# One PSUM bank moved from the input projections to the transposes of the band attention's first two blocks

## The chip, the cores and the metric

The kernel runs on one core of one Trainium2 chip. The metric is device microseconds (us) of one execution; of several executions the median is taken. The kernel before takes 3063.79 us (median of 3 executions, 3062.14 to 3065.21).

## The reference

One inference step of a one-layer streaming encoder, over 2048 prompt tokens and 32 sample tokens (model width 1024). Attention has two groups: group A is differential attention over all earlier keys, group B is band attention in chunks of 64 frames, each of which sees itself and the eight chunks before it. The band attention of the prompt:

```python
qa, ka, va, qb, kb, vb = split_proj(rmsnorm(hp, g_attn[i]), w_in[i])
oa = diff_attn_prompt(qa, ka, va, t5_table, lam)
ob = band_attn_prompt(qb, kb, vb, band_table[i])
hp = hp + merge(oa, ob, subln_g[i], out_norm_b[i], w_out[i], lam_init)
hp = ffn_ple(hp, p_prompt[i], g_mlp[i], w_up[i], w_down[i], w_ple_gate[i], w_ple_proj[i])
...
def band_core(q, k, v, bias, mask):
    s = jnp.einsum('bqhd,bkhd->bhqk', q, k).astype(jnp.float32) * (HEAD_DIM ** -0.5) + bias[None]
    s = jnp.where(mask, s, NEG)
    p = jax.nn.softmax(s, axis=-1)
    return jnp.einsum('bhqk,bkhd->bqhd', p.astype(v.dtype), v)
```

Everything is fp32. The kernel splits each operand into a high and a low part and adds three products (high by high, high by low, low by high), so a product of depth 1024 is 24 matmuls.

## The kernel before, in words

**Blocks and stages.** Tokens are handled in four blocks b = 0 to 3 of 512 (the last has 544: 512 prompt tokens and the 32 sample tokens). `proj` (L443) makes the q, k and v of a group: `vtile` (L411) makes a 128x256 piece of v (tile `vps`, 24 matmuls of 256 columns, read out by ScalarE at L427), the loop at L451 to L502 makes a piece of q or k (tile `qps`, 24 matmuls of 512 columns, for b = 3 two tiles of 272 columns each; read out by VectorE at L475 or L480). q, k and v are written to DRAM and read back by the attention. `run` writes the stages down in this order: projections of blocks 0 and 1, attention A of the first 1024 queries (`attn_a`), group B's projections of blocks 0 and 1, band attention of its first two blocks, group B's projections of block 2 and of block 3, band attention of its last two blocks, group A's projections of blocks 2 and 3 (`proj_a`), then the norm of the band attention's outputs (`onorm`, two of them woven into the end of `proj_a`), the load of the normed attention outputs of block 0 (`oload`), attention A of the last queries, the output projections (`outproj`, tile `ops`) and the MLP (tiles `ups` and `dps`).

**What sets the order.** The kernel is built with a scheduler (`schedule_with_timeline_sim=True`). The order in which the program is written is only a priority: on each engine the scheduler places what its own estimate of time says is ready, the earlier-written first. Once placed, each engine's instructions run in that order, and so do the DMA issues, which all stand on SyncE's queue (SP). So projections written later stand between the attention's instructions on TensorE (PE) as filler.

**Band attention.** `attn_b` (L715) is called for four blocks `JB` of the queries: (0, 1), (2, 3), (4, 5) and (6, 7, 8). It runs over 8 heads; a head has four tiles of 128 queries (the last block also the 32 sample queries). For each query tile `first` (L796) does the scores (tile `sb`, L804; two banks of 320 keys where there are 640, two matmuls each), bias and maximum on VectorE (L807), the exponential and the scaling on ScalarE (L812, L814). `second` (L817) transposes the 128x640 weights on PE (tile `tpb`, L826: five transposes in two banks, four and one), copies each bank out as a high part on ScalarE (L834) and a low part on VectorE (L835), and after two query tiles `attn_b_out` (L842) multiplies by the values (tile `ob`, L856) and adds up into `t` (L859 to L861), which is written to the DRAM tensor `oT` once per head. From the second block on, a head has 16 matmuls into `sb`, 20 into `tpb` and 12 into `ob`, so counts of `sb` matmuls are used below to say how far the band attention is: the first block ends at 64, the second at 192, all four at 464.

**What follows the projections.** `onorm` (L868) reads the four `oraw` tiles of a block back from `oT`, squares them on ScalarE (L875, L877) and adds; `colnorm2` sums over partitions with two matmuls (tile `css`, L1046 and L1047), makes the factor `r` (L1050 to L1056) and writes it to DRAM (`rB`). `oload` (L881) reads eight `oraw` tiles of block 0, multiplies the last four by `rb` (read from `rB`; L902) and splits each into the operands `oact` and `ou` of the output projection (ScalarE L181, VectorE L187). The buffers of `oact` lie where the projections' activations lay, so they come free when the projections that read these are done; the `oraw` buffers are a ring of three.

**PSUM.** There are 8 banks: two in the pool `mm` (`mz`), one in the pool `mmx`, two for scores (`ps_s`), two for transposes (`ps_t`), one for outputs (`ps_o`), all eight in use. `Rings` (L109) is an object with a `tile` method that takes the next pool of its list at each call. `mm` is such a ring over `mz`, `mz` and `mmx`: everything that is given `mm` goes through three banks.

## Time and profile before

| what | value |
|---|---|
| median of 3 executions | 3063.79 us |
| the profiled execution's own time | 3069.65 us |
| its span, first to last instruction | 3067.9 us |
| PE busy in the span | 2947.2 us |
| VectorE, ScalarE, GpSimd busy | 1830.6, 1746.5, 1887.9 us |
| mean granted TensorE clock | 0.985 |

In the views shown below, a row of the table by stretches gives the stretch in us from the span's start and its length, then for each engine its busy time and its number of instructions in brackets (PE matmuls, PEld weight loads, DVE VectorE, ACT ScalarE, POOL GpSimd), the granted clock of TensorE as a share of full speed, the busy share of the DMA engines and GB/s. With a tile's name only that tile's PE instructions are counted. A row of the order of time has the start, the duration, the engine, the line, the operation, what is written and read, the form, how many rows were merged, and in brackets the idle time before it with what ended that. A matmul's busy time overlaps the next one's, so sums of matmul durations are more than the time they take.

### The profile page before, as it was taken

The page shows a single profiled execution, that of the slowest core. Times are in us where ns is not written, and L with a number is a line of the kernel's source. Part 1 is how long each engine was busy: PE and PEld are TensorE (multiplying, and loading weights), DVE is VectorE, ACT ScalarE, POOL GpSimd, SP SyncE. Part 2 cuts the span into 40 slices and gives each one's busy share as a digit, 9 for nine tenths or more (in the row PEclk, how much of TensorE's full clock was granted, in tenths as well). Part 3 has the DMA queues.
Part 4 walks back from the last instruction along what each step waited for, and adds up shares of the span by engine and source line. Part 5 has one row for each costly group of instructions (what it writes and reads, how often), then busy time and mean ns, then how long its engine had stood idle before and what let it go on. Part 6 is the DMA issues. An engine that isn't in the chain of part 4 may idle for free. (4 is left out here: it accounts for less than half of the span.)

```text
span 3067.9 us, 50404 instructions
## 1 busy us (share of the span) xinstructions
PE 2947.2 (96%) x17409; PEld 2599.0 (85%) x17409; DVE 1830.6 (60%) x4233; ACT 1746.5 (57%) x3234; POOL 1887.9 (62%) x2509
## 2 busy tenths in 40 slices
PE   7999999899789999999999999999899999999997
PEld 6788889899677888888888888879798888999997
DVE  5156554654655555566666565545677885577664
ACT  5256554765666666566666565554555545555455
POOL 3467775324146544656655565777688888787774
PEclk9999999999899999999999999999999999999999
DMA  9878866976687554455655543347433446333331
GB/s 310 250 222 245 241 221 211 262 228 211 190 248 241 147 148 131 145 155 172 198 149 155 150 128 125 118 148 249 136 131 117 148 151 231 122 101 112 102 99 57
DMA packets 298119, 529.54 MB, mean 173 GB/s; under 512 B 36668, under 2 KB 161632, under 8 KB 297864
## 3 DMA queue, kind: packets, MB, share of 16 engines
q1 hardware_dynamic: 297864, 526.32, 55.6%
q8 instruction: 138, 2.26, 0.3%
q14 instruction: 117, 0.96, 0.1%
HBM read 425.19 MB, written 104.97 MB: 173 GB/s over the span
## 5 line engine op out<-in xcount | busy, mean ns | idle before, releaser
L176 POOL TENSOR_TENSOR wl<-wr,wh 128x256 fp32r<-128x256 f32 x648 | 492.8, 792 | 270.2 <-ACT wh L181 230.7
L181 ACT ACTIVATE piece<-wr 128x512 fp32r<-128x512 f32 x406 | 245.8, 625 | 290.4 <-PE ups L220 133.3
L176 POOL TENSOR_TENSOR piece<-wr,piece 128x256 fp32r<-128x256 f32 x404 | 338.0, 863 | 92.3 <-ACT piece L181 85.2
L181 ACT ACTIVATE wh<-wr 128x1024 fp32r<-128x1024 f32 x228 | 240.5, 1055 | 190.8 <-PE ups L220 45.9
L166 POOL TENSOR_TENSOR wl<-wr,wh 128x256 fp32r<-128x256 f32 x264 | 202.9, 799 | 208.4 <-ACT wh L181 202.6
L219 PE MATMUL dps<-uh,piece 128*128 128x272 f32 (+1 forms) x768 | 247.0, 325 | 8.3 <-ACT piece L181 5.0
L221 PE MATMUL dps<-uh,piece 128*128 128x272 f32 (+1 forms) x768 | 247.3, 325 | 1.1 <-POOL piece L166 0.9
L220 PE MATMUL dps<-ul,piece 128*128 128x272 f32 (+1 forms) x768 | 248.1, 324 | 0.1
L166 POOL TENSOR_TENSOR piece<-wr,piece 128x256 fp32r<-128x256 f32 x280 | 235.1, 872 | 18.9 <-ACT piece L181 15.4
L219 PE MATMUL ups<-cs,piece 128*128 128x256 f32 (+1 forms) x864 | 246.2, 285 | 0.0
L221 PE MATMUL ups<-cs,piece 128*128 128x256 f32 (+1 forms) x864 | 246.1, 285 | 0.0
L220 PE MATMUL ups<-cs,piece 128*128 128x256 f32 (+1 forms) x864 | 245.9, 285 | 0.0
L219 PE MATMUL qps<-aH,wh 128*128 128x512 f32 (+1 forms) x640 | 226.9, 355 | 2.0 <-DVE ql L475 2.0
L220 PE MATMUL qps<-aL,wh 128*128 128x512 f32 (+1 forms) x640 | 227.9, 356 | 0.0
L221 PE MATMUL qps<-aH,wl 128*128 128x512 f32 (+1 forms) x640 | 226.5, 354 | 0.0
L1112 DVE TENSOR_TENSOR h<-h,dps 128x512 f32<-128x512 f32 x256 | 173.5, 682 | 80.2 <-PE dps L221 77.0
L638 ACT ACTIVATE e<-e,nm 128x128 f32<-128x128 f32 (+16 forms) x136 | 157.2, 1156 | 108.5 <-DVE nm L636 108.0
L1155 DVE TENSOR_TENSOR h<-h,dps 128x272 f32<-128x272 f32 (+1 forms) x384 | 189.0, 514 | 42.9 <-PE dps L221 42.3
L219 PE MATMUL dps<-uh,wh 128*128 128x512 f32 x512 | 205.7, 402 | 0.6 <-DVE h L1112 0.6
L219 PE MATMUL ups<-cH,wh 128*128 128x512 f32 x512 | 202.5, 396 | 0.0
L221 PE MATMUL ups<-cH,wl 128*128 128x512 f32 x512 | 202.2, 395 | 0.1
L220 PE MATMUL ups<-cL,wh 128*128 128x512 f32 x512 | 202.0, 394 | 0.0
(307 smaller groups left out, 9234.0 us busy)
## 6 DMA issues: line engine op xcount, KB each, us to landing
wr<-w_up SPq DMA_DIRECT2D x128, 512.0 KB, 3.5
wr<-w_down SPq DMA_DIRECT2D x128, 512.0 KB, 3.6
v<-vSa SPq DMA_DIRECT2D x64, 512.0 KB, 4.6
q<-qS SPq DMA_DIRECT2D x128, 256.0 KB, 5.2
wr<-w_qk SPq DMA_DIRECT2D x50, 512.0 KB, 5.2
ka<-kS SPq DMA_DIRECT2D x32, 512.0 KB, 7.1
wr<-w_out SPq DMA_DIRECT2D x32, 512.0 KB, 4.8
wr<-w_ple_gate SPq DMA_DIRECT2D x32, 512.0 KB, 3.5
```

Of the source, the lines that this page charges most:

```text
L166: nc.gpsimd.tensor_tensor(out[:, sl], a[:, sl], b[:, sl], op=op)
L176: nc.gpsimd.tensor_tensor(out[:, sl], a[:, sl], b[:, sl], op=op)
L181: nc.scalar.activation(hi, raw, AF.Copy)
L219: nc.tensor.matmul(ps, lh, rh, start=start and i == 0, stop=False)
L220: nc.tensor.matmul(ps, lh, rl, start=False, stop=False)
L221: nc.tensor.matmul(ps, ll, rh, start=False, stop=stop and i == n - 1)
L638: nc.scalar.activation(row, row, AF.Exp, bias=nmx, accum_out=z[:nr, m : m + 1])
L1112: nc.vector.tensor_tensor(hv, hv, ps, op=ALU.add)
L1155: nc.vector.tensor_tensor(hv, hv, ps, op=ALU.add)
```

## The change

```diff
-            mm = Rings((mz, "mm"), (mz, "mm"), (opened(mmx, "mmx", 1, PSUM), "mm"))
+            third = opened(mmx, "mmx", 1, PSUM)
+            mm = Rings((mz, "mm"), (mz, "mm"), (third, "mm"))
...
+            tb = Rings((ps_t, "tp"), (ps_t, "tp"), (third, "mm"))
             for js in JB[: len(JB) // 2]:
-                self.attn_b(js, bp, ps_s, ps_t, ps_o)
-            weave(self.proj((2,), 1, acts, sg, mm), lifted(self.prep(3, acts, pp, mm, "mm")), 3)
+                self.attn_b(js, bp, ps_s, tb, ps_o)
+            weave(self.proj((2,), 1, acts, sg, mz), lifted(self.prep(3, acts, pp, mz, "mm")), 3)
             ppx.close()
             self.rawp = Rings((self.wp, "wr"))
             self.caches(sg, tp)
-            drain(self.proj((3,), 1, acts, sg, mm))
+            drain(self.proj((3,), 1, acts, sg, mz))
...
             def proj_a():
-                yield from self.proj(HALVES[1], 0, acts, sg, mm, gs=range(GS))
+                yield from self.proj(HALVES[1], 0, acts, sg, mz, gs=range(GS))
                 for b in HALVES[1]:
-                    yield from self.proj((b,), 0, acts, sg, mm, vs=(), gs=range(GS, 4))
+                    yield from self.proj((b,), 0, acts, sg, mz, vs=(), gs=range(GS, 4))
```

In the first two blocks of the band attention (64 query tiles, 96 tiles `tpb`) every third `tpb` goes to the third bank. The projections of blocks 2 and 3, group B's and group A's, and the `rp` tiles of block 3 use the two banks of `mz` alone. The last two blocks of the band attention keep two banks for transposes, and `onorm`, `outproj` and all later stages keep `mm` with three. No instruction is added or removed: both programs have 17404 matmuls on PE, 576 of them into `tpb`, 1920 into `qps`, 1632 into `vps`.

The scheduler places the instructions anew from the stage of attention A's first queries on. Until the band attention begins, the counts are nearly the same (at 16 `sb` matmuls, 1248 `qps` matmuls stand ahead before and 1243 now). Then they part. How many matmuls of each kind stand ahead of a given `sb` matmul on PE:

| `sb` matmuls | `vps` before, now | `qps` before, now | `ops` before, now |
|---|---|---|---|
| 48 | 1309, 1302 | 1344, 1344 | 0, 0 |
| 96 | 1616, 1585 | 1344, 1344 | 0, 0 |
| 112 | 1632, 1632 | 1438, 1364 | 0, 0 |
| 144 | 1632, 1632 | 1668, 1485 | 0, 0 |
| 176 | 1632, 1632 | 1897, 1606 | 0, 0 |
| 192 | 1632, 1632 | 1920, 1671 | 0, 0 |
| 224 | 1632, 1632 | 1920, 1809 | 0, 0 |
| 240 | 1632, 1632 | 1920, 1920 | 72, 0 |
| 320 | 1632, 1632 | 1920, 1920 | 384, 384 |

At the end of the band attention 432 `ups` and 378 `dps` matmuls stood ahead before, 394 and 336 now; at the last matmul of attention A it was 1536 and 1445, now 1488 and 1397. The rows near the end of the program are the same again.

**The end of the projections on PE.** Before, from the last `qps` matmuls on:

```order
L221 MATMUL qps<-aH,wl 128x272
L1046 MATMUL css<-sh,ones_r 128x512
L1047 MATMUL css<-sl,ones_r 128x512
L804 MATMUL sb<-kbt,q 128x320 x4
L856 MATMUL ob<-pb,vbt 128x512 x4
L856 MATMUL ob<-pb,vbt 128x2x128
L826 MATMUL tpb<-ident,eb 128x128 x4
L856 MATMUL ob<-pb,vbt 128x2x128
L826 MATMUL tpb<-ident,eb 128x128
L804 MATMUL sb<-kbt,q 128x320 x4
L826 MATMUL tpb<-ident,eb 128x128 x5
```

Band attention alone goes on like this until 48 `sb`, 59 `tpb` and 36 `ob` matmuls have passed; only then comes the first `ops`. The same place now:

```order
L221 MATMUL qps<-aH,wl 128x272
L804 MATMUL sb<-kbt,q 128x320 x2
L1047 MATMUL css<-sl,ones_r 128x512
L804 MATMUL sb<-kbt,q 128x320 x2
L1046 MATMUL css<-sh,ones_r 128x512
L826 MATMUL tpb<-ident,eb 128x128 x5
L1047 MATMUL css<-sl,ones_r 128x512
L219 MATMUL ops<-oact,wh 128x512
L804 MATMUL sb<-kbt,q 128x320 x4
L220 MATMUL ops<-oact,wh 128x512
```

The first `ops` stands 12 matmuls behind the last `qps`, and both blocks' `css` stand between them (block 0's first one is the exception: it stands some 240 matmuls earlier, its partner L1047 here). After the first `ops` come in turn 4 `sb`, 26 `ops`, a query tile's `ob` and `tpb`, 9 `ops`, two query tiles of the band attention with 3 `ops` between, and then 24 `ops` in a row.

**The end of the second block on SP's queue** (`t_6463` is the output of its last head). Before:

```order
L157 DMA oT<-t_6327 64x512
L157 DMA kbt<-kS 64x1024 x2
L157 DMA q<-qS 64x1024
L157 DMA bb<-dbb 128x640
L157 DMA q<-qS 64x1024
L157 DMA vbt<-vSb 128x8x128
L157 DMA oT<-t_6463 64x512
L157 DMA oraw<-oT 128x512 x3
L157 DMA kbt<-kS 64x1024 x2
```

Now:

```order
L157 DMA oT<-t_6463 64x512
L157 DMA ka_pt<-kr 128x512
L157 DMA kbt<-kS 64x1024 x2
L157 DMA bb<-dbb 128x640
L157 DMA q<-qS 64x1024 x2
L157 DMA kS<-qh 128x512
L157 DMA kS<-ql 128x512
L157 DMA oraw<-oT 128x512 x3
```

Now results of the projections (`ka_pt`, `kS`) are still being written when the second block's last output goes out, and the three `oraw` loads that open the way to the output projection stand behind them.

## The prediction

> **What bounds the kernel now.** I read the page first, then the stretches of the band attention, then who waited there. The page's first lines and its rows of PE and of the clock in 40 slices:

> ```profile
> span 3067.9 us, 50404 instructions
> PE 2947.2 (96%) x17409; PEld 2599.0 (85%) x17409; DVE 1830.6 (60%) x4233; ACT 1746.5 (57%) x3234; POOL 1887.9 (62%) x2509
> PE   7999999899789999999999999999899999999997
> PEclk9999999999899999999999999999999999999999
> ```

> PE is the bound almost everywhere. The change removes no work, so it can only win or lose where PE stands idle or runs at a lowered clock. The eleventh slice (767 to 844 us) is the weak one in the part that the change touches: least busy, and the only digit of the clock under 9. The stretches around it:

> ```profile
> 608.20:644.50 36.30, 35.07 (x267) 33.68 (x267) 22.59 (x87) 23.48 (x51) 4.51 (x10) 0.98 0.85 244
> 669.30:770.00 100.70, 100.70 (x654) 92.73 (x653) 45.84 (x164) 57.92 (x117) 43.00 (x67) 1.00 0.70 210
> 776.00:826.00 50.00, 32.89 (x131) 24.32 (x130) 28.71 (x105) 31.82 (x67) 5.70 (x13) 0.75 0.65 192
> 860.00:890.00 30.00, 23.67 (x114) 19.98 (x113) 14.91 (x44) 16.28 (x30) 16.62 (x25) 0.89 0.91 281
> 890.00:1010.00 120.00, 110.81 (x534) 90.28 (x533) 68.10 (x188) 79.47 (x147) 72.31 (x101) 0.99 0.78 232
> ```

> From 669 to 770 us PE is never idle. From 776 to 826, between the last projection and the first output projection, it is idle for 50.00 - 32.89 = 17.1 us of 50 and has a clock of 0.75: band attention stands there without filler. Call this the hole. PE's waits before it (515 to 776 us, two rows) and in it (776 to 826, three rows):

> ```profile
> PE sb L804 <- DVE stb L807: 5.8, 4, 2.2
> PE tpb L826 <- DVE pb L835: 1.0, 1, 1.0
> ```

> ```profile
> PE ob L856 <- DVE pb L835: 7.3, 3, 6.6
> PE sb L804 <- DVE stb L807: 7.0, 11, 0.9
> PE tpb L826 <- DVE pb L835: 2.4, 2, 1.6
> ```

> Waiting for a bank of the transposes cost PE 1.0 us in 261 us beside the projections. The third bank's direct worth is therefore about nothing. What counts is the order that comes with it.

> **Term 1: the old hole, +30 us.** How long PE needs for the hole's work, if fed, comes from the stretches of `qps` alone (two pure ones, wide and narrow, then the mixed one) and the count of `sb` in two stretches:

> ```profile
> 100.00:120.00 20.00, 20.00 (x88) 1.00 1.05 353
> 515.80:522.80 7.00, 7.00 (x58) 1.00 0.89 239
> 669.30:770.00 100.70, 81.03 (x461) 1.00 0.70 210
> ```

> ```profile
> 669.30:770.00 100.70, 13.47 (x65) 1.00 0.70 210
> 776.00:826.00 50.00, 12.21 (x44) 0.75 0.65 192
> ```

> A 512-column matmul takes 20/88 = 0.227 us, a 272-column one 7/58 = 0.121. `proj_a` has 24 wide for 48 narrow ones, 0.156 on average. So the 461 `qps` took 71.9 us of the 100.7, and the 65/16 = 4.06 heads of band attention beside them 28.8: 7.1 us a head. The hole's 44/16 = 2.75 heads are 19.5 us of work in 50: 30 us are lost, 17.1 idle and the rest as slower matmuls. Now 556 `qps` stand between the 112th and the 240th `sb`, where before 482 ended at the 177th. That fills these heads, so I take all 30 off; at least the 17.1 of idle goes.

> How the clock follows the idle time shows around an earlier, smaller gap:

> ```profile
> 603.00:606.40 3.40, 1.40 (x12) 1.19 (x11) 1.90 (x9) 2.85 (x9) 1.80 (x5) 1.00 0.83 274
> 606.40:609.80 3.40, 3.40 (x14) 2.83 (x13) 1.68 (x6) 1.30 (x4) 3.40 (x5) 0.51 0.11 30
> ```

> After 3.4 us with PE 1.40 busy, the next 3.4 us run at 0.51, although the longest single wait between 515 and 776 us was 2.2: here it is the idle share that lowers the clock, not one long gap. [...]

> **Term 2: the new hole, -13 us.** Now both `css` come at the very end of the projections, and block 0's output projection needs `r` from them for the last four of its eight operands. The chain, from the trace of before (block 0's `css` and its `r`, then block 1's; the two transfers; the first use of `rb` and the first `ops` behind it):

> ```profile
> 773.47 0.39 PE L1047 MATMUL css<-sl,ones_r 128*128 128x512 f32 x1
> 782.89 0.69 DVE L1056 TENSOR_TENSOR r<-r,sqacc 128x512 f32<-128x512 f32 x1
> 831.06 0.60 ACT L1050 ACTIVATE sqacc<-css 128x512 f32<-128x512 f32 x1 [0.75 <-PE css L1047]
> 843.89 0.67 DVE L1056 TENSOR_TENSOR r<-r,sqacc 128x512 f32<-128x512 f32 x1
> 835.09 0.75 DVE L902 SCALAR_TENSOR_TENSOR oraw<-oraw,g_b_s,rb 128x512 f32<-128x512 f32 x1 [0.19 <-DMA rb<-rB]
> 840.79 0.50 PE L220 MATMUL ops<-oact,wh 128*128 128x512 f32 x1 [0.79 <-DVE oact L187]
> ```

> ```profile
> rB<-r SPq DMA_DIRECT2D x3, 256.0 KB, 2.0
> rb<-rB SPq DMA_DIRECT2D x3, 256.0 KB, 3.5
> rB<-r SPq DMA_DIRECT2D x1, 272.0 KB, 5.8
> rb<-rB SPq DMA_DIRECT2D x1, 272.0 KB, 5.4
> ```

> From `css` to `r` it took 9.7 and 13.5 us, writing and reading 2.0 + 3.5 (5.8 + 5.4 the slow ones), from L902 to `ops` 5.7: 20.9 to 24.7 us. Meanwhile PE's order has, before the run of 24 `ops` that needs `rb`, 39 `ops` at 0.227 = 8.9 us and some 3.25 query tiles at 7.1/4 = 5.8, with `css` 15.2. That leaves 5.7 to 9.5 us idle. VectorE stands at L902 too, so the band attention cannot fill it. The old hole lost 30 us for 17.1 idle, 1.75 times; so 10.0 to 16.6, and I take 13. Bounds: 5.7 if the clock stays up, and with the slow transfers (15.2 idle) 26.6.

> **Term 3: thinner filler, -5 us.** Between the 112th and 240th `sb` a head now has 69.5 `qps`, 10.8 us, and takes 10.8 + 7.1 = 17.9 us instead of about 25. The nearest row is 608.20:644.50: 32 `sb`, two heads, 18.15 us each with `vps` as filler, 36.30 - 35.07 = 1.23 us idle. So 0.6 us a head, 8 heads: 4.9 us, where the full heads of 669 to 770 lost nothing. Bounds 0 and twice that. ScalarE and VectorE were 23.48 and 22.59 busy of 36.30 there, so neither is the bound at this pace.

> **Term 4: two banks for the projections, -2 us.** With two, PE fills one while the other is read out. A read-out on VectorE or ScalarE takes:

> ```profile
> L475 DVE SCALAR_TENSOR_TENSOR ql<-qps,rbt x14: 422/434/692, 541.9 to 766.9; 128x272 f32<-128x272 f32 x10, 128x512 f32<-128x512 f32 x4
> L427 ACT ACTIVATE vraw<-vps,rcol x18: 448/472/478, 567.8 to 649.3; 128x256 f32<-128x256 f32 x16, 32x256 f32<-32x256 f32 x2
> ```

> ```profile
> L219 PE MATMUL qps<-aH,wh 128*128 128x512 f32 (+1 forms) x640 | 226.9, 355 | 2.0 <-DVE ql L475 2.0
> ```

> The shortest tile keeps PE busy for 24 x 0.121 = 2.9 us, six times a read-out, so only a queue on the reading engine can hold PE up. With three banks the 640/8 = 80 `qps` tiles lost 2.0 us. 84 tiles now have two: 2.1 us at the same rate. Bounds: 0, and a whole read-out each, 84 x 0.45 = 38 us. I stay at the row, since VectorE was 45.84 busy of 100.70.

> Behind 890 us I cost the change at nothing: PE is the bound there, the 96 MLP matmuls that now come after attention A have MLP as neighbours, and the waits of 860 to 1010 us (6.3 + 9.2 idle) come from loads and ScalarE's order in the output projection, which can fall either way by a few us.

> **Sum.** 30 - 13 - 5 - 2 = 10 us. The profiled execution took 3069.65 us (its span 3067.9), so it would be 3059.6; it lies 5.9 us above the median of 3063.79, and against that median the forecast is **3053.7 us**.

> **Rivals.** *The hole moves.* If the new hole costs its upper 26.6 us, the rest is 30 - 26.6 - 7 = -4 to +3 us: about 3061 to 3067. For it: the chain of 20.9 us and more is all in one piece, and ScalarE and VectorE now do both blocks' factors in between. Against it: 39 `ops` were placed ahead of the wait. *Two banks make bubbles.* If the read-outs queue behind ScalarE's exponentials and each of the 84 tiles waits one read-out, 38 us go: 30 - 13 - 5 - 38 = -26, 3090 us. It is slower than before from (10 + 2)/84 = 0.14 us a tile on, and slower by over 0.2% from 0.22. For it: PE is at 100.70 of 100.70, so every bubble is lost; against it: the 2.0 us of 80 tiles. [...] *The order does nothing*: if the heads on the chip keep their old 25 us and PE waits, 8 x 7 = 56 us would go; the row of 608.20 with 18.15 us a head speaks against it, and I give it no chance of its own beyond that of bubbles.

> **How the numbers follow.** Forecast, 6 to 24 us faster: 0.57 (0.10 of it with one dip only). The hole moves, within 6 us: 0.26. Bubbles: 0.17. The measurement can tell 0.2%, 6.1 us, from no change, so faster, same and slower have these chances. The low end is 30 - 5.7 - 0 - 0 = 24 us faster, 3040; the high end takes in the moved hole, 3067, and leaves out the bubbles.

> **What would show it.** Right: the 50 us from the 177th to the 221st `sb` have PE busy and the clock at 1.0; `sb` 112 to 240 take about 18 us a head; a hole of 6 to 10 us idle, with a dip of the clock, stands where the first `ops` begin, with `ops` or L902 waiting for `rb`. Wrong: PE waits at `qps` or `vps` for L475, L480 or L427 of more than some us in all; `sb` waits for L807 of more than 1 us a head; or new waits behind 890 us that are larger than 15 us in all.

## The result, and the profile after

The changed kernel takes **3043.12 us** (median of 4 runs, 3040.56 to 3050.62) where the kernel before takes 3064.50 (4 runs beside it, 3062.14 to 3065.92): a ratio of 0.9933, 95% interval 0.9919 to 0.9947. A second comparison on another chip gave 3049.87 against 3064.12, ratio 0.9950 (0.9937 to 0.9963). So it is faster by 14 to 21 us, and the forecast of 10 us was five to seven tenths of that. The profiled execution took 3040.56 us.

The page of the changed kernel, its first lines and the rows of PE and of the clock in 40 slices:

```profile
span 3038.8 us, 50386 instructions
PE 2935.5 (97%) x17409; PEld 2588.7 (85%) x17409; DVE 1827.7 (60%) x4233; ACT 1744.8 (57%) x3234; POOL 1887.9 (62%) x2509
PE   7999999999899999999999999999899999999997
PEclk9999999999999999999999999999999999999999
```

PE's eleventh slice has gone from 7 to 8, the eighth and the twelfth from 8 to 9, and the clock has no digit under 9. The stretches of the band attention: two early heads, the eight heads from the 112th to the 240th `sb`, then the new hole and what follows:

```profile
598.90:634.50 35.60, 33.29 (x257) 31.97 (x257) 23.08 (x85) 25.01 (x54) 7.36 (x14) 1.00 0.80 237
651.50:796.10 144.60, 143.35 (x934) 131.59 (x933) 83.59 (x309) 101.91 (x211) 54.66 (x89) 1.00 0.80 231
796.10:826.00 29.90, 23.55 (x108) 18.20 (x107) 22.93 (x62) 20.09 (x41) 5.27 (x7) 0.94 0.80 237
860.00:890.00 30.00, 24.00 (x104) 19.41 (x104) 17.92 (x44) 17.66 (x32) 19.37 (x26) 0.89 0.78 250
```

The eight heads take 144.60/8 = 18.1 us each (17.9 forecast) with 1.25 us of PE idle in all and the clock at 1.00. The hole that was 17.1 us idle has become one of 29.90 - 23.55 = 6.4. What PE waited for, beside the projections (515 to 796 us, first fence) and behind them (796 to 1010 us):

```profile
PE tpb L826 <- DVE pb L835: 2.0, 4, 0.7
PE qps L219 <- DVE ql L475: 1.8, 2, 1.4
PE sb L804 <- DVE stb L807: 0.3, 1, 0.3
```

```profile
PE ops L219 <- ACT oact L181: 6.1, 4, 2.4
PE ops L219 <- DVE hd L926: 4.4, 2, 4.1
```

In the new hole it is the output projection that waits, twice for more than 2 us. Below each of the two PE rows stands the row that held it up, one of ScalarE and one of VectorE:

```profile
808.83 1.65 PE L219 MATMUL ops<-oact,wh 128*128 128x512 f32 x3 [2.39 <-ACT oact L181]
808.15 0.63 ACT L181 ACTIVATE oact<-oraw 128x512 fp32r<-128x512 f32 x1 [2.74 <-DMA oraw<-oT]
819.86 0.97 PE L219 MATMUL ops<-oact,wh 128*128 128x512 f32 x3 [2.34 <-ACT oact L181]
818.40 2.08 DVE L902 SCALAR_TENSOR_TENSOR oraw<-oraw,g_b_s,rb 128x512 f32<-128x512 f32 x3 [1.50 <-DMA rb<-rB]
```

Only the second wait goes back to `rb`: block 0's second `css` (L1047) began at 795.46 us, and 24.4 us later the `ops` that needed it went on (20.9 to 24.7 forecast). The first wait is for an `oraw` load, which the forecast did not have in its chain; in the second profile of this kernel the two waits are 2.68 and 3.38 us, with ScalarE 3.67 us at an `oraw` load ahead of the first.

So far nearly all looks like the forecast. To see where the time went, I cut each profile at five marks and worked out from the records of PE and of the clock what was **lost** in each part: PE's idle time plus half of the time that it was busy at half clock. What is left of the span is the work, 2914 to 2920 us in every kernel below but `e1`, so the losses account for the differences. Two profiles each of the kernel before, of `e2` (an experiment) and of the changed one:

| us lost | before | again | `e2` | again | changed | again |
|---|---|---|---|---|---|---|
| start to first `sb` | 36.7 | 33.9 | 34.3 | 35.8 | 31.5 | 36.6 |
| to last `qps` | 10.9 | 11.0 | 6.6 | 6.4 | 9.6 | 9.4 |
| to first `ops` (old hole) | 26.0 | 24.4 | 15.1 | 16.5 | 0.5 | 0.0 |
| to first `ups` | 16.6 | 21.7 | 15.4 | 16.5 | 21.3 | 25.8 |
| to the last `o` of attention A | 6.7 | 7.7 | 4.0 | 9.0 | 9.2 | 10.0 |
| to the end | 54.4 | 51.7 | 50.0 | 52.3 | 48.9 | 49.8 |
| all | 151.3 | 150.5 | 125.4 | 136.7 | 121.0 | 131.6 |

Two profiles of one kernel differ by up to 11 us in all and 5 in a part, so only what both show counts. The old hole is gone for good (25.2 us on average to 0.3). By the means 4.4 come back behind it, up to the first `ups`, but there the profiles of the two kernels overlap (21.7 before, 21.3 now). Both profiled executions of the kernel before (3069.65 and 3066.07 us) were slower than its median, so the table has 24.6 us between before and changed where the medians have 14 to 21.

### The profile page after: what moved, and what is told of

Read it like the earlier page. It is cut to its first block, busy times and chain, and to the rows that moved or that the text cites. A ratio compares the mean times of both kernels' runs of the same rounds, so it can differ in the third digit from the quotient of the medians.

```text
span 3038.8 us, 50386 instructions
## 1 busy us (share of the span) xinstructions
PE 2935.5 (97%) x17409; PEld 2588.7 (85%) x17409; DVE 1827.7 (60%) x4233; ACT 1744.8 (57%) x3234; POOL 1887.9 (62%) x2509
## 5 line engine op out<-in xcount | busy, mean ns | idle before, releaser
L219 PE MATMUL dps<-uh,piece 128*128 128x272 f32 (+1 forms) x768 | 246.6, 325 | 7.5 <-ACT piece L181 4.1
L220 PE MATMUL dps<-ul,piece 128*128 128x272 f32 (+1 forms) x768 | 247.5, 324 | 0.0
L219 PE MATMUL ups<-cs,piece 128*128 128x256 f32 (+1 forms) x864 | 245.5, 284 | 0.0
L220 PE MATMUL ups<-cs,piece 128*128 128x256 f32 (+1 forms) x864 | 245.3, 284 | 0.0
L219 PE MATMUL qps<-aH,wh 128*128 128x512 f32 (+1 forms) x640 | 226.4, 354 | 2.8 <-DVE ql L475 2.8
L220 PE MATMUL qps<-aL,wh 128*128 128x512 f32 (+1 forms) x640 | 226.4, 354 | 0.0
L219 PE MATMUL dps<-uh,wh 128*128 128x512 f32 x512 | 206.2, 403 | 4.4 <-DVE h L1112 4.4
L220 PE MATMUL ups<-cL,wh 128*128 128x512 f32 x512 | 201.8, 394 | 1.6 <-POOL cL L166 0.8
L219 PE MATMUL ups<-cH,wh 128*128 128x512 f32 x512 | 202.0, 395 | 0.9 <-ACT relu L1083 0.9
## 6 DMA issues: line engine op xcount, KB each, us to landing
q<-qS SPq DMA_DIRECT2D x128, 256.0 KB, 5.6
```

The source lines that it names most:

```text
L219: nc.tensor.matmul(ps, lh, rh, start=start and i == 0, stop=False)
L220: nc.tensor.matmul(ps, lh, rl, start=False, stop=False)
```

## The experiments

At first I held that the gain comes from **the order** that the third bank of the transposes brings (projections as filler up to the 240th `sb`), and not from the bank itself or from fewer banks for the projections.

**Half of the change: projections on two banks, transposes on two.** From the changed kernel:

```diff
             for js in JB[: len(JB) // 2]:
-                self.attn_b(js, bp, ps_s, tb, ps_o)
+                self.attn_b(js, bp, ps_s, ps_t, ps_o)
```

> Projections on two banks, transposes on two as before: the third bank is used by neither beside the projections. The program's order is about that of before (176 sb matmuls ahead of the last qps, 224 ahead of the first ops, as before). Theory (the gain comes from the order, which keeps projections as filler): no gain, 3062 to 3069 us, the loss being the 2 us of 84 tiles at the old rate of waits; a hole of about 15 us idle between the last qps and the first ops stands as before. Rival 1 (fewer banks for the projections are good by themselves): near 3043. Rival 2 (two banks make bubbles, which the new order happens to hide): 3075 to 3100, with PE waiting at qps or vps for L475, L480 or L427 by 10 us or more.

Measured: 3045.50 us (5 runs) against 3065.71, ratio 0.9941 (0.9927 to 0.9955), as the first rival had it. The theory fell: without any third bank for the transposes, and with the order of before (48 `sb` without filler), nearly all of the gain is there. Its stretches from the first `sb` to the last `qps`, and from there to the first `ops`, and the second of these in the kernel before:

```profile
522.70:766.00 243.30, 238.39 (x1662) 223.63 (x1663) 132.68 (x498) 161.40 (x363) 87.59 (x145) 0.99 0.80 237
766.00:807.90 41.90, 30.38 (x143) 22.19 (x143) 28.47 (x105) 31.44 (x67) 7.29 (x15) 0.91 0.84 238
```

```profile
773.40:825.50 52.10, 34.99 (x147) 26.16 (x145) 28.86 (x107) 33.92 (x71) 7.26 (x15) 0.76 0.66 192
```

The same 48 `sb` without filler take 41.90 instead of 52.10 us. One row of ScalarE stands out, here in the kernel before and in `e2`:

```profile
792.95 0.63 ACT L877 ACTIVATE oraw<-oraw 128x512 f32<-128x512 f32 x1 [7.21 <-DMA oraw<-oT]
```

```profile
782.70 0.63 ACT L877 ACTIVATE oraw<-oraw 128x512 f32<-128x512 f32 x1 [1.85 <-DMA oraw<-oT]
```

Before, ScalarE stood 7.21 us at L877 for a load of the second block's last output, with the exponentials of the band attention queued behind it; in `e2` 1.85. In the kernel before the clock was then at half for 17.1 us in one piece. The new theory (A in the expectations): this one stand is worth some 10 us, and the two banks only happened to move it away.

The changed kernel has such a stand as well, but with projections beside it PE is not idle for a moment:

```profile
767.59 0.63 ACT L877 ACTIVATE oraw<-oraw 128x512 f32<-128x512 f32 x1 [3.60 <-DMA oraw<-oT]
755.00:775.00 20.00, 20.00 (x122) 17.94 (x121) 9.83 (x39) 13.38 (x26) 8.16 (x14) 1.00 0.89 270
```

**The third bank for one block alone**, on the same chip: the second block (64 of the 96 `tpb`), then the first (32).

```diff
-                self.attn_b(js, bp, ps_s, tb, ps_o)
+                self.attn_b(js, bp, ps_s, tb if js == JB[1] else ps_t, ps_o)
```

> The changed kernel with the third bank for the transposes of the second block alone (64 of the 96 tiles). Its order is about that of the changed kernel (240 sb ahead of the last qps, 244 ahead of the first ops). Theory (order): all of the gain, 3041 to 3047 us. Rival (the third bank's own worth, by tiles): two thirds of the gain of 20.5 us, 3051.

> The changed kernel with the third bank for the transposes of the first block alone (32 of the 96 tiles). Its order is about that of before (176 sb ahead of the last qps, 224 ahead of the first ops). Theory (order): no gain, 3060 to 3068 us, with the old hole of about 15 us idle ahead of the first ops. Rival (the third bank's own worth, by tiles): a third of the gain, 3057.

Measured: 3048.55 us, ratio 0.9947 (0.9935 to 0.9960), and 3053.48, ratio 0.9962 (0.9950 to 0.9975; with `JB[0]` in the diff). Neither theory holds. `e10` has the filled hole (1.8 us lost there) and `e11` the old one (14.4 lost), yet both gain 12 us or more; both have the projections on two banks. Beside the projections they lose 13.5 and 11.0 us, no less than the kernel before, so what `e2` gains there does not come with the two banks alone. Why `e11` takes 8 us more than `e2` is open.

**The stand of ScalarE alone.** The kernel before, with the squares of blocks 0 and 1 on GpSimd, so that ScalarE has no L877 to stand at:

```diff
-                nc.scalar.activation(raw, raw, AF.Square)
+                if b in HALVES[0]:
+                    self.pool_tt(raw, raw, raw, ALU.mult)
+                else:
+                    nc.scalar.activation(raw, raw, AF.Square)
```

> The kernel before, with one edit: the squares of the output's norm for blocks 0 and 1 (L877) are taken by GpSimd instead of ScalarE, so that ScalarE cannot stand at L877 for an oraw load. Banks and counts stay as before (176 sb matmuls ahead of the last qps, 224 ahead of the first ops). Theory A (in the old hole one stand of ScalarE of 7.21 us, with the half clock behind it, cost about 10 us, and the projections' two banks only happened to take it away): the stretch from the last qps to the first ops shrinks from 52.1 us to 41 to 44, and the time falls by 8 to 12 us, to 3053 to 3058. Rival B (two banks for the projections gain by their own pace): no change, 3062 to 3068. Rival C (GpSimd is now late with the factors): slower than 3068.

Measured: 3063.02 us (11 runs) against 3064.63, ratio 0.9999 (0.9990 to 1.0007): no change. But the hole did what theory A said, as its stretch shows, with the one from the first `ups` to the last `o` below it, and then PE's two largest waits in that second stretch and a row of VectorE:

```profile
768.50:810.40 41.90, 31.73 (x143) 23.03 (x141) 28.49 (x108) 32.34 (x69) 8.19 (x18) 0.88 0.82 235
955.00:1937.80 982.80, 970.27 (x4987) 817.06 (x4985) 584.78 (x1512) 601.08 (x1010) 546.16 (x774) 1.00 0.51 151
```

```profile
PE sb L804 <- DVE stb L807: 5.1, 1, 5.1
PE o L696 <- DMA v<-vSa: 3.2, 3, 2.4
971.42 0.75 DVE L951 SCALAR_TENSOR_TENSOR tmp<-tmp,g_mlp_s,rl 128x512 f32<-128x512 f32 x1 [4.82 <-DMA tmp<-hS]
```

From 52.10 to 41.90 us: the stand was worth 10 us there. Then 15.3 us are lost from the first `ups` to the last `o` (12.5 of them idle in the row), where the two profiles of before lose 6.7 and 7.7. The largest piece is a stand of the same kind on VectorE, 4.82 us at L951 for a load, with L807 of the band attention's last queries queued behind it. The edit had moved the scheduler's order there too: 1488 `ups` and 1397 `dps` matmuls stand ahead of the last `o`, where before it was 1536 and 1445. The five other profiles with 1488 (two of the changed kernel, and those of `e10`, `e3` and `g1` below) lose 8.0 to 16.1 there, the seven with 1536 4.0 to 9.0. So theory A is right for the hole and wrong for the time: of 9.9 us won in the hole, 8.1 went again behind the first `ups`. This is one profile, and the account does not close. In all it loses 141.8 us, 9 less than the kernel before on average; its work is 4 more, and the rest lies in how far the profiled executions are from their medians.

**A second profile of the kernel before**, unchanged.

> The kernel before once more, unchanged, for a second profile. Theory A: the same 7 us stand of ScalarE at L877 and the hole of 50 to 53 us from the last qps to the first ops are there again, while the small differences elsewhere (the start up to the first sb of 525.0 us, the stretch to the 96th sb of 119.5) move by a few us either way. If the stand is missing in this profile and the time is still about 3064, theory A falls.

Measured: 3066.07 us; the stand is there with 4.15 us, the hole is 49.8 us long and loses 24.4. As theory A has it; the half clock lasts 20.5 us in one piece.

**The other half of the change: transposes on three banks, the projections still on all three.** In the four lines of the projections:

```diff
-            weave(self.proj((2,), 1, acts, sg, mz), lifted(self.prep(3, acts, pp, mz, "mm")), 3)
+            weave(self.proj((2,), 1, acts, sg, mm), lifted(self.prep(3, acts, pp, mm, "mm")), 3)
```

> The other half of the change alone: transposes of the first two blocks on three banks, the projections on three banks as before, the third shared by both. The shared bank ties the order: no projection of the later parts can be placed ahead of the first two blocks (at 16 sb 816 vps and 768 qps stand ahead instead of 1248 qps, and 340 sb ahead of the last qps, 342 ahead of the first ops). All theories: the first two blocks run without filler, 192 sb or 12 heads of which 8 had filler before; at 14 us a head alone against 7.1 with filler about 50 to 60 us more, 3110 to 3130. If it came near 3045 the order would count for nothing.

Measured, in one run: 3158.22 us, 94 more than before, and more than expected. With the third bank shared, no projection can run ahead of the transposes that own the bank before it. Attention A loses its filler as well, which I had left out. Its stretches of attention A up to the first `sb` and of the second block, and the first of these in the kernel before:

```profile
520.10:597.90 77.80, 67.73 (x369) 51.11 (x369) 68.66 (x286) 75.61 (x174) 2.61 (x18) 0.99 0.75 198
172.00:471.00 299.00, 251.98 (x1421) 215.43 (x1420) 180.60 (x497) 166.88 (x339) 176.71 (x246) 0.89 0.66 193
```

```profile
172.00:525.00 353.00, 345.76 (x2239) 312.29 (x2237) 212.48 (x556) 203.84 (x398) 256.93 (x354) 1.00 0.76 229
```

47.0 us idle against 7.2, at a clock of 0.89. So the two halves belong together in this sense only: the projections must leave the third bank before the transposes can take it.

**Filler in the hole by another way**: transposes on two banks, all of group A's projections of blocks 2 and 3 on the third bank alone, which spreads them up to the 212th `sb`. The expectation speaks of their last part, but the edit changes the second `self.proj` of `proj_a` in the same way, and the pieces of v go through the one bank as well.

```diff
-                yield from self.proj(HALVES[1], 0, acts, sg, mz, gs=range(GS))
+                yield from self.proj(HALVES[1], 0, acts, sg, Rings((third, "mm")), gs=range(GS))
```

> The transposes keep two banks; the last part of group A's projections (24 qps tiles) has one bank, the third, alone, the other projections have two. 212 sb matmuls stand ahead of the last qps and 224 ahead of the first ops, so that 12 instead of 48 are left without filler. Theory A (what is worth time is the order around the hole, whatever bank brings it): 3040 to 3050 us, as the changed kernel, or up to 12 us more if each of the 24 tiles waits 0.5 us for its read-out. Rival B (only a third bank for the transposes lets the order pay): 3060 or more.

Measured: 3061.63 us (11 runs) against 3064.63, ratio 0.9989 (0.9979 to 1.0000). The hole is as good as gone (3.5 us lost), but from the first `sb` to the last `qps` 22.3 are lost. PE's largest wait there is for read-outs of v, and the row below it is what stands ahead of the longest of these:

```profile
PE vps L219 <- ACT vraw L427: 8.6, 4, 3.3
630.30 0.63 ACT L877 ACTIVATE oraw<-oraw 128x512 f32<-128x512 f32 x1 [2.75 <-DMA oraw<-oT]
```

PE waits at the place that the second rival named, but not for a queue of exponentials. Ahead of each of the four read-outs ScalarE stood for a transfer: 2.75 and 2.73 us at L877, 1.43 at L875, and 2.92 at the read-out itself until a piece of v was written. A hole closed at this price is worth some 3 us at most. It decides nothing between the theories: 3061.6 lies within A's upper end and in B's range.

**Both again, on one chip**, the changed kernel and `e2`.

> The changed kernel once more, unchanged, on one chip with e2_again, for what the transposes' third bank adds to two banks for the projections. Theory D (the filled hole saves 15 us beside e2, and waits in the output projection and in attention A give back all but some 4): 0.05 to 0.2% faster than e2_again, 3041 to 3046 us; idle plus half-clock losses in the profile: hole under 2, last qps to first ups over 18, first ups to the end of attention A over 8. Rival E (the third bank is most of the gain, the first comparison was chance): faster than e2_again by 10 us or more.

> Projections on two banks, transposes on two, once more, unchanged. Theory D: 3043 to 3048 us, 0 to 6 us behind after_again, with a hole of 40 to 44 us from the last qps to the first ops, in which about 15 us are lost, and 4 to 6 us lost from the first ups to the end of attention A. Rival E: 3053 or more.

Measured: 3049.87 us and 3047.59, ratios to before 0.9950 (0.9937 to 0.9963) and 0.9950 (0.9937 to 0.9964). Rival E falls: beside two banks for the projections, the third bank of the transposes adds nothing that can be measured. Theory D has most of the losses right, but not the time of the changed kernel, which came out 2 us behind `e2` and not ahead of it. The table says why. From `e2` to the changed kernel the hole loses 15.6 us less (means of two profiles: 15.8, 0.3), and 3.0 more are lost beside the projections, 7.6 more up to the first `ups`, 3.1 more in attention A: 13.7 of 15.6 given back (the last of the three lies within the scatter). The rows of the third of these in the changed kernel and in `e2`:

```profile
797.60:944.40 146.80, 131.96 (x617) 108.00 (x618) 83.88 (x227) 88.02 (x164) 73.36 (x105) 0.95 0.81 241
```

```profile
807.90:944.90 137.00, 126.88 (x608) 105.49 (x607) 77.30 (x219) 85.98 (x160) 68.70 (x102) 0.95 0.81 244
```

14.8 us idle against 10.1: the output projection now waits for `rb` and `oact` as described above, and both kernels come to their first `ups` at the same time (944.4 and 944.9 us; 953.1 and 948.2 in the second pair), the changed one with 316 `sb` done against 296.

**The row sums earlier**, in the kernel before and, ahead of it, in the changed one (`ONP` sets where in group A's projections the output's norm is begun and where its `css` follow):

```diff
-ONP = (28, 1, 6)
+ONP = (28, 1, 4)
```

> The kernel before with the row sums of the output's norm begun earlier (third number of ONP 4 instead of 6), banks and counts as before (176 and 224 sb). Theory D (each reordering moves a handful of waits of 2 to 10 us; what decides is whether ScalarE stands at L877 in the old hole): the stand goes if the loads fall earlier, then 3052 to 3060; if it stays, 3062 to 3068. Rival F (only two banks for the projections gain): 3062 to 3068 in either case.

> The changed kernel with the row sums of the output's norm (css) begun earlier in the weave with group A's projections (the third number of ONP 4 instead of 6), so that block 0's factor is known before the projections end; 54 instead of 39 ops stand ahead of the 256th sb. Theory (what is left in the new hole, 6.4 us idle and one step of 3.4 us at half clock, comes from the chain css, r, rB, rb): the first ops run goes on without that wait, 4 to 8 us less than the changed kernel, 3035 to 3040. Rival (the hole is ScalarE's and VectorE's work on the output projection itself, oact and hd): no gain, 3041 to 3046.

Measured: in the kernel before 3060.42 us against 3064.12, ratio 0.9988 (0.9979 to 0.9996). The stand stays (3.79 us) and so does the hole (20.4 lost); of the expectations "it stays" is the nearer, 2 us off. In the changed kernel 3040.39 us against 3065.71, ratio 0.9916 (0.9903 to 0.9930), at the edge of what was expected. Both long waits of the new hole are gone, but later ScalarE stands 8.60 us for an `oraw` load:

```profile
850.47 0.63 ACT L181 ACTIVATE oact<-oraw 128x512 fp32r<-128x512 f32 x1 [8.60 <-DMA oraw<-oT]
```

**And four buffers for these loads** instead of three, on top of `e3`:

```diff
-        self.nt = 3
+        self.nt = 4
```

> e3_onp_early (the changed kernel with earlier row sums) with four instead of three buffers for oraw, hd and the squares in the first part of the output projection, so that the oraw loads are issued one tile earlier. Theory (ScalarE's and VectorE's waits for oraw loads are what is left there): 2 to 8 us less than e3, 3032 to 3038. Rival (the loads are late because of SP's queue, not of the buffers): no gain, 3038 to 3043.

Measured: **3039.11 us** (5 runs, 3036.82 to 3039.90) against 3064.12, ratio 0.9917 (0.9903 to 0.9930); on the same chip the changed kernel took 3049.87. So on this chip this version beats both kernels. Against `e3` nothing more is shown, though the place did change:

```profile
800.50:931.90 131.40, 121.98 (x594) 101.40 (x595) 79.02 (x208) 81.96 (x153) 75.99 (x105) 0.99 0.84 254
931.90:1914.50 982.60, 969.70 (x4972) 815.20 (x4970) 581.74 (x1505) 599.52 (x1008) 542.55 (x773) 1.00 0.50 151
```

Up to the first `ups` 9.4 us are idle at a clock of 0.99, with 11.1 lost the least of all kernels; up to the last `o` 12.9 are idle, with 16.1 lost the most. Once more the gain of one stage was given back in a later one.

## Why the prediction was right in sign and wrong in cause

The time lies in the stated range, but for a cause that the forecast did not have, so the range held partly by luck.

- **Term 1** (the old hole, +30): right in mechanism. The hole's loss went from 25.2 us to 0.3, and with projections beside it even a stand of 3.60 us at L877 costs PE nothing. But of these 25, 9.4 go without any filler (`e2`), by an order in which ScalarE no longer stands 4 to 7 us at L877. I had read PE's gap of 6.6 us in that hole as want of filler; its row named `pb`, and following that back leads to ScalarE, where the stand is.
- **Term 2** (the new hole, -13): the place, the length of the chain (24.4 us) and the idle time in all (6.4) came out as forecast. But only 2.34 us of that idle time wait for `rb`; 2.39 wait for an `oraw` load that the chain did not have, so the sum is right partly by luck. With one stretch at half clock (3.42 us, 1.7 lost) it cost 8, 1.27 times the idle time and not 1.75. And it is not a pure addition: the kernel before lost 16.6 and 21.7 us in this stage by its own waits; the net is 4.4 by the means, within the scatter.
- **Term 3** (thinner filler, -5): 18.1 us a head as forecast, but 1.25 us idle instead of 4.9. The 1.23 us idle of the row that I scaled were one wait for `stb` (L807), and such waits fell from 5.8 us to 0.3 beside the projections.
- **Term 4** (two banks for the projections, -2) is **the step that failed**. The cost was sized rightly (`qps` waited 1.8 us), but I took this edit for a price only. Alone it gains 16.5 and 20.2 us: 4.5 beside the projections, 9.4 in the hole and 3.2 in the output projection by the means of the table, the last within the scatter. "What counts is the order that comes with it" was right, but it was this edit's order and not the third bank's.
- **The third bank's direct worth, "about nothing"**: right beside the projections, and shown by the pair of runs. Where there is no filler it was not tested (below).
- **Behind 890 us, nothing**: as good as right. By the means 2.4 more are lost in attention A and 3.7 less to the end, where two profiles of one kernel differ by up to 5.0 and 2.7.
- **How the clock falls**: I read the two rows at 603 us as the work of many short gaps. PE's idle time in the first of them is one gap of 2.00 us, for `wl`; a dip behind two gaps of 0.85 and 0.59 us is shown only further below.

The size came out low since 13 + 5 + 2 were charged where 4.4 - 1.5 were due by the means. Not settled: why the scheduler, with two banks for the projections, sets L877 some instructions later on ScalarE and loses less beside the projections. That these losses shrink in both profiles of `e2` is shown; that they would in another kernel is not. Nor is it shown which one move gives the time: `f1` shortened the hole by as much as `e2` and gained nothing.

## What to carry to other kernels

Where a change has two halves, run each alone: here the half that looked like the price was the gain, and what the other half won by closing the hole was paid back in other stages. Account for each stage as idle time plus lowered clock, in two profiles of each kernel, before a gain in one stage is believed. And follow a gap to the engine that stands in order, not just to the product that was late: one load that ScalarE waited for was worth 10 us in its stage.

## What the runs showed of the hardware

```profile
787.36:790.78 3.42, 1.06 (x5) 0.59 (x4) 0.95 (x5) 0.00 (x0) 0.00 (x0) 1.00 0.85 277
790.78:794.19 3.41, 0.00 (x0) 0.00 (x0) 0.00 (x0) 1.24 (x2) 0.53 (x1) 0.50 0.95 236
794.19:797.60 3.41, 1.95 (x5) 1.56 (x6) 1.27 (x5) 3.18 (x8) 1.17 (x4) 0.50 0.38 96
797.60:801.02 3.42, 2.73 (x12) 2.31 (x11) 1.67 (x6) 1.28 (x4) 0.00 (x0) 0.50 0.17 49
801.02:804.43 3.41, 2.82 (x12) 2.25 (x11) 2.65 (x12) 2.53 (x6) 0.00 (x0) 0.50 0.51 143
804.43:807.84 3.41, 3.34 (x12) 2.58 (x11) 0.20 (x2) 1.97 (x4) 0.00 (x0) 0.50 0.00 0
```

PE's gap of 6.64 us behind the stand reaches into three of these intervals; behind the next two, with 0.69 and 0.59 us idle, one wait for `stb` each, the clock was still at half, and behind the one with 0.07 it was full. In this piece of 17.1 us PE is busy for 10.8, so it costs 5.4. In the whole hole the half clock cost 8.9, 10.4 and 9.0 us in the three profiles with a stand of 4 to 7 us, and 2.9 to 5.1 in the four where the stand was 2.3 us or less or there was none (`e2` twice, `e11`, `f1`). Four intervals of the changed kernel around the first wait of its new hole:

```profile
802.00:805.42 3.42, 3.42 (x17) 2.82 (x16) 1.18 (x3) 3.42 (x7) 0.41 (x3) 1.00 1.05 293
805.42:808.83 3.41, 1.03 (x9) 0.75 (x7) 2.10 (x5) 0.65 (x2) 0.00 (x0) 1.00 0.98 283
808.83:812.25 3.42, 3.42 (x8) 2.74 (x9) 3.42 (x12) 1.16 (x4) 0.00 (x0) 0.50 1.05 359
812.25:815.66 3.41, 2.71 (x16) 1.99 (x16) 3.21 (x11) 2.38 (x5) 0.00 (x0) 1.00 0.89 302
```

One wait of 2.39 us, one interval at half with PE busy for all its 3.42 us, and back. In the kernel before, two gaps of 0.85 and 0.59 us in one interval (777.10 to 780.51 us, PE 1.96 busy of 3.41) stood ahead of the dip at 780.5 us (780.51 to 783.92 us at 0.50).

**In `e1`, with three banks for the transposes, band attention alone keeps ScalarE busy nearly all the time.** In the row of `e1`'s second block, ScalarE is busy 75.61 of 77.80 us, and a head takes 77.80/8 = 9.7 us; with two banks in `e2` the heads without filler take 14.0 (41.90/3), ScalarE busy 31.44 of 41.90, partly with the output's norm. The blocks are not the same and the output's norm runs in one of them only, so this does not show what the third bank is worth there.
